# Norms, weight splits and broadcasts of a two-model fp32 forward pass, moved and regrouped

## The chip, the core and the metric

The program runs on one core of a Trainium2 chip. The metric is device time in microseconds, the median of several executions. Five engines matter here: TensorE (PE, with its weight loads shown as PEld), VectorE (DVE), ScalarE (ACT), GpSimd (POOL) and SyncE (SP), which issues most DMAs.

## What is computed

A sequence of 512 positions with 1024 channels goes through two blocks of two layers each, all in float32. Every layer mixes positions and then applies a gated feed-forward part with a short depthwise convolution:

```python
h = rmsnorm(x, pre); y = mixer(h); x = x + rmsnorm(y, post)
h = rmsnorm(x, ffn_pre); y = conv_ffn(h); x = x + rmsnorm(y, ffn_post)
```

The mixers of the first block are three attention or pooling branches with gates. Those of the second block are a convolution module and, in the last layer, dilated attention over three groups whose keys and values come from `rmsnorm(x, kv_norm_g) @ w_kv`. There the norm's gain is multiplied into the weights instead of into the activations.

## The kernel before, in words

**Products.** Every float32 product is made of three fp32r products: each operand is split in a high part (a rounded copy) and a low part (the difference), and high*high, high*low and low*high are added in PSUM (`mm3`, L329 to L331, and `mm3_rows`, L515 to L517).

**Weights.** All weights lie in one array of 500 units of 128x1024 floats in the order of use (`PLAN`). `dma_to` (L270) loads units through SP into three buffers `raw`. `split_to` (L278) splits a unit: ACT writes the high part (L299), DVE the low part (L300), into one of four buffers `w` or, for units marked keep, one of four buffers `keep`. A unit with a gain (72 units, all of the dilated stage) is first scaled in place by POOL (L296). `take_units` (L310) asks for loads up to three units ahead and for splits up to two ahead.

**Closings.** Each of the eight parts ends in `closing` (L573): the output product, then the norm, the residual addition and the next norm. It works in two halves of 256 positions, each of two tiles of 128. For half 0 it takes eight units of weights and fills four PSUM banks, then starts `norms(0)`; while that runs on DVE, ACT and POOL, PE computes half 1 with the same units; then `norms(1)` starts, and `head` begins the first six products of the next part with the normalised half 0. `head`'s first four units are keep units.

**The norm.** `norms` (L388) adds the bank to y (DVE, L398, or L401 with a bias), squares and sums it (ACT, L386), and, where there is an addition or a bias, multiplies y by the gain on POOL (L407, four 128x512 pieces per half). `rms` (L374) is a chain of twelve small DVE instructions (L379, L380, L351, then L355 to L357 three times). The residual goes into x on DVE (L413). `pre_norm` (L424) then squares x (L386), runs `rms` again, scales x into xn (ACT L441 for the first tile, DVE L437 for the second), and after a yield PE transposes xn (L448, tile `htp`) and ACT and DVE split the transposed tiles into hh and hl (L678, L679; L455, L456 without a gain), two tiles of 128 channels at a time.

**Order.** Side work is written as generators; a yield gives the time, in a clock kept while the program is built, after which the rest is issued. The framework then orders the instructions of each engine by a model of their times: among those ready in the model, the one issued first goes first. So an instruction of low priority can stand in the queue ahead of one of high priority that was not yet ready in the model. On the chip each queue runs in that order.

**Start.** `run` (L1563) issues on SP: half 0 of x, ident, vecs (562 KB of per-channel vectors), two units of weights, half 1 of x, a third unit, and small tables. Two small DVE instructions make `hb` from vecs (L1592). Then `pre_norm` of both halves and the first head.

**Dilated stage.** For each of eight heads `dilated_merge` (L1459) computes two softmax weights in small DVE and ACT steps (L1484 to L1492), yields 3.6, and PE then broadcasts them to a PSUM tile `dwb` (L362, four transposes).

Of the kernel before, what the change touches and what calls it, by code (L numbers as in the profile page):

```python
# [25 lines left out]
OP = mybir.AluOpType  # L26
# [204 lines left out]
class Kernel:  # L231
    def __init__(self, tc, t, out, stop=None):
        self.tc, self.nc, self.t, self.out, self.stop = tc, tc.nc, t, out, stop
        self.n_unit = self.n_dma = self.n_split = 0
        self.raws, self.units = {}, {}
        self.keep = None
        self.headed = []
        self.lanes, self.clock, self.ticking = [], 0.0, False
# [31 lines left out]
    def dma_to(self, n):  # L270
        while self.n_dma < min(n, len(PLAN)):
            u = self.n_dma
            raw = self.wp.tile([P, UNIT, P], F32, tag="raw", name=f"raw{u}", bufs=RAW_BUFS)
            self.nc.sync.dma_start(raw, self.t["wall"][u].rearrange("p (i m) -> p i m", m=P))
            self.raws[u] = raw
            self.n_dma += 1

    def split_to(self, n):  # L278
        nc = self.nc
        while self.n_split < min(n, len(PLAN)):  # L280
            u = self.n_split
            tiles, keep, gain = PLAN[u]
# [9 lines left out]
            if gain is not None:  # L292
                g = self.vec("kv_norm_g" if gain == "kv" else "mix_pre_g1")
                k0, n = tiles[0][2], len({k for _, _, k, _ in tiles})
                rows = raw.rearrange("p (k i) m -> p k (i m)", k=n)
                nc.gpsimd.tensor_tensor(  # L296
                    rows, rows, g[:, k0 : k0 + n, None].to_broadcast(list(rows.shape)), op=OP.mult
                )
# [3 lines left out]
            self.n_split += 1  # L302

# [70 lines left out]
    def rms(self, sums):  # L374

        nc = self.nc
        v = self.sm.tile([P, 2], F32, tag="var", name="var", bufs=2)
        y = self.sm.tile([P, 2], F32, tag="rst", name="rst", bufs=4)
# [9 lines left out]
    def norms(self, h, banks, y, add, gain, bias, pre):  # L388
# [4 lines left out]
        for i in range(2):  # L393
            for n in range(2):
# [27 lines left out]
        yield from self.pre_norm(h, pre)  # L422

    def pre_norm(self, h, gain, wait=(0.0, 0.0)):  # L424
# [9 lines left out]
        for i in range(2):  # L434
            xn.append(self.sp.tile([P, D], F32, tag="xn", name="xn", bufs=2))
            if i:
                nc.vector.tensor_scalar(  # L437
                    xn[i], self.x[:, 2 * h + i], rs[:, i : i + 1], None, op0=OP.mult
                )
            else:  # L440
                nc.scalar.activation(xn[i], self.x[:, 2 * h + i], AF.Copy, scale=rs[:, i : i + 1])  # L441
        yield NORM_SUM[h] + NORM_NEXT
        at = slice(h * HS, (h + 1) * HS)
        for f in range(0, KD, 2):
# [128 lines left out]
    def closing(self, w, l, xs, y, gain, pre, bias=None, ready=None, begun=None):  # L573
# [6 lines left out]
        with self.tc.tile_pool(name="tail", bufs=1, reuse_waits="tile") as tp:  # L580
# [8 lines left out]
            done = len(units)  # L589
            for k in range(done, KD):  # L590
# [7 lines left out]
            self.spawn(self.norms(0, banks, y, add, gain, bias, pre))  # L598
            banks = [[self.psum(tag, "mm") for tag in tags] for tags in (("a", "a"), ("a", "b"))]
            order = (4, 5, 6, 7, 0, 1, 2, 3)  # L600
            self.close_some(xs, units, banks, 1, order, every, 4, 3)
# [857 lines left out]
    def dilated_merge(self, hd):  # L1459
# [33 lines left out]
        yield 3.6  # L1493
# [69 lines left out]
    def run(self):  # L1563
        nc, tc, t = self.nc, self.tc, self.t
        with ExitStack() as st:
# [12 lines left out]
            nc.sync.dma_start(self.vecs, t["vecs"])  # L1578
# [4 lines left out]
            self.load_x(1)  # L1583
            self.dma_to(RAW_BUFS)
# [5 lines left out]
            self.hb = cst.tile([P, 48], F32, name="hb")  # L1590
            for l in range(2):
                nc.vector.tensor_scalar(  # L1592
                    self.hb[:, 24 * l : 24 * l + 24], self.vec(f"b_gate{l}"), 0.5, None, op0=OP.mult
                )
            self.new_h()
            with tc.tile_pool(name="start", bufs=1, side="right") as sp:
# [5 lines left out]
                self.keep = None  # L1602
            for n, stage in enumerate(self.stages()):
# [126 lines left out]
```

## Time and profile before

| | |
|---|---|
| median of 3 runs | 3212.48 us (3210.5 to 3213.6) |
| profiled execution | 3215.7 us, of which 3213.9 us is the span of the program's instructions |
| PE busy | 3114.8 us, 97% of the span |
| DVE, ACT, POOL busy | 1853.6, 1349.2, 423.2 us |
| mean granted TensorE clock | 0.990 |

A timeline row gives the start in us from the span's beginning, the duration, engine, line, operation, what is written <- what is read, the shape and count, and in brackets the engine's idle time before it and what ended that. Durations of matmuls overlap, since they are pipelined. The granted clock has two levels here, 1.0 (2.4 GHz) and 0.5 (1.2 GHz).

### The profile page before, as it was taken

The numbers are of one execution on the slowest core, as the hardware profiler recorded it, in microseconds if no ns is written. First come the engines' busy times: TensorE is split into PE (matmuls) and PEld (weight loads), VectorE is DVE, ScalarE is ACT, GpSimd is POOL, SyncE is SP. The second block draws the span as 40 slices with busy tenths as digits, with TensorE's granted clock in tenths as the row PEclk, the third lists the DMA queues.
The fourth block names the chain that finished last, engine by engine and source line by source line (L and its number), as shares of the span: only waits on it lengthen the run. The fifth ranks groups of instructions, "written<-read, shape, count | busy, mean of one in ns | idle before, by whom it ended". The sixth has DMA issues, their size and how long they took to land.

```text
span 3213.9 us, 40538 instructions
## 1 busy us (share of the span) xinstructions
PE 3114.8 (97%) x15764; PEld 2617.7 (81%) x15764; DVE 1853.6 (58%) x3310; ACT 1349.2 (42%) x2183; POOL 423.2 (13%) x414
## 2 busy tenths in 40 slices
PE   8999999999999999999999899999899999999998
PEld 7787878888778788888878778888788888888886
DVE  5778356446676854645467855445545545474555
ACT  4566345334456643434343244333333333353332
POOL 0223110000111322000000010000333334100001
PEclk9999999999999999999999999999999999999999
DMA  3222232232221223223334422223222222223322
GB/s 137 66 69 74 99 113 78 97 99 94 95 66 59 76 93 109 77 97 98 99 107 144 157 66 83 95 99 105 66 86 79 72 79 79 79 86 97 97 95 72
DMA packets 86687, 292.26 MB, mean 91 GB/s; under 512 B 10976, under 2 KB 15840, under 8 KB 86496
## 3 DMA queue, kind: packets, MB, share of 16 engines
q1 hardware_dynamic: 83040, 276.84, 26.2%
q10 hardware_dynamic: 3456, 12.85, 1.1%
q8 instruction: 124, 2.03, 0.3%
q14 instruction: 67, 0.55, 0.1%
HBM read 286.23 MB, written 2.10 MB: 90 GB/s over the span
## 4 chain that ended last, share of the span: by engine, by line
PE 82%; DVE 10%; ACT 4%; issue 2%; DMA 1%; SPq 1%; POOL 0%; ACTq 0%; DVEq 0%; POOLq 0%
PE mm L331 18%; PE mm L330 18%; PE mm L329 18%; PE mm L515 6%; PE mm L517 6%; PE mm L516 6%; ACT junk L386 2%; DVE w L300 2%; PE z L329 1%; PE z L331 1%; PE z L330 1%; PE htp L448 1%; DVE cacc L1279 1%; PE pt L876 1%; PE dpo L1440 1%
## 5 line engine op out<-in xcount | busy, mean ns | idle before, releaser
L329 PE MATMUL mm<-hh,w 128*128 128x512 f32 (+1 forms) x2720 | 1052.9, 387 | 0.0
L330 PE MATMUL mm<-hl,w 128*128 128x512 f32 (+1 forms) x2720 | 1036.1, 381 | 0.0
L331 PE MATMUL mm<-hh,w 128*128 128x512 f32 (+1 forms) x2720 | 1035.7, 381 | 0.0
L300 DVE TENSOR_TENSOR w<-raw,w 128x1024 fp32r<-128x1024 f32 x436 | 563.1, 1292 | 444.7 <-ACT w L299 440.3
L331 PEld LDWEIGHTS mm<-hh,w 128*128 128x128 f32 x2720 | 512.1, 188 | 96.9 <-issue 1.4
L330 PEld LDWEIGHTS mm<-hl,w 128*128 128x128 f32 x2720 | 512.8, 189 | 90.0 <-issue 2.2
L329 PEld LDWEIGHTS mm<-hh,w 128*128 128x128 f32 x2720 | 512.6, 188 | 89.8 <-issue 1.7
L299 ACT ACTIVATE w<-raw 128x1024 fp32r<-128x1024 f32 x436 | 458.9, 1053 | 237.8 <-PE mm L517 187.6
L629 DVE SCALAR_TENSOR_TENSOR cg<-mm,vecs,cg 128x511 f32<-128x511 f32 (+1 forms) x176 | 131.9, 750 | 212.8 <-ACT cg L622 209.9
L407 POOL TENSOR_TENSOR y<-y,row 128x512 f32<-128x512 f32 x40 | 53.9, 1373 | 1339.6 <-ACT junk L386 1339.6
L516 PE MATMUL mm<-w,ah 128*128 128x512 f32 x576 | 226.2, 393 | 0.0
L515 PE MATMUL mm<-w,ah 128*128 128x512 f32 x576 | 225.9, 392 | 0.0
L517 PE MATMUL mm<-w,al 128*128 128x512 f32 x576 | 225.7, 392 | 0.0
L296 POOL TENSOR_TENSOR raw<-raw,vecs 128x1024 f32<-128x1024 f32 x72 | 147.7, 2051 | 568.2 <-DMA raw<-in_wall 516.2
L629 DVE SCALAR_TENSOR_TENSOR cv<-mm,vecs,cv 128x511 f32<-128x511 f32 (+1 forms) x176 | 132.0, 750 | 100.1 <-ACT cv L622 97.3
L622 ACT ACTIVATE cg<-mm,vecs 128x512 f32<-128x512 f32 x88 | 68.7, 781 | 286.3 <-PE mm L331 286.1
L330 PE MATMUL mm<-hl,keep 128*128 128x256 f32 x512 | 144.7, 285 | 7.0 <-DVE hl L679 7.0
L331 PE MATMUL mm<-hh,keep 128*128 128x256 f32 x512 | 144.0, 283 | 0.0
L329 PE MATMUL mm<-hh,keep 128*128 128x256 f32 x512 | 143.8, 287 | 0.2
L515 PEld LDWEIGHTS mm<-w,ah 128*128 128x128 f32 x576 | 109.0, 189 | 23.3 <-issue 0.8
L516 PEld LDWEIGHTS mm<-w,ah 128*128 128x128 f32 x576 | 109.1, 189 | 22.5
L517 PEld LDWEIGHTS mm<-w,al 128*128 128x128 f32 x576 | 109.0, 189 | 22.5
(285 smaller groups left out, 4445.4 us busy)
## 6 DMA issues: line engine op xcount, KB each, us to landing
raw<-in_wall SPq DMA_DIRECT2D x500, 512.0 KB, 3.5
cw<-in_cm_mats ACTq DMA_DIRECT2D x20, 576.0 KB, 6.6
row<-in_rows SPq DMA_DIRECT2D x9, 512.0 KB, 4.2
x<-in_x SPq DMA_DIRECT2D x4, 512.0 KB, 7.2
bt<-in_rpb SPq DMA_DIRECT2D x16, 128.0 KB, 2.0
cup<-cu SPq DMA_DIRECT2D x80, 16.0 KB, 1.8
out<-x SPq DMA_DIRECT2D x4, 256.0 KB, 2.1
out<-x ACTq DMA_DIRECT2D x4, 256.0 KB, 2.1
```

What stands on the lines that cost most here:

```text
L296: nc.gpsimd.tensor_tensor(rows, rows, g[:, k0 : k0 + n, None].to_broadcast(list(rows.shape)), op=OP.mult)
L299: nc.scalar.activation(hi, raw, AF.Copy)
L300: nc.vector.tensor_tensor(lo, raw, hi.bitcast(F32), op=OP.subtract)
L329: nc.tensor.matmul(ps, wh, xh, start=first and i == 0, stop=False, **check)
L330: nc.tensor.matmul(ps, wh, xl, start=False, stop=False, **check)
L331: nc.tensor.matmul(ps, wl, xh, start=False, stop=stop, **check)
L386: self.nc.scalar.activation(junk, x, AF.Square, accum_out=total)
L515: nc.tensor.matmul(ps, xh, wh, start=first, stop=False)
L516: nc.tensor.matmul(ps, xh, wl, start=False, stop=False)
L517: nc.tensor.matmul(ps, xl, wh, start=False, stop=last)
L622: nc.scalar.activation(o, ps, AF.Identity, scale=self.vec(taps + str(k0), f), bias=self.vec(cb, f))
L629: nc.vector.scalar_tensor_tensor(o[:, to], ps[:, of], self.vec(taps + str(k), f), o[:, to], op0=OP.mult, op1=OP.add,)
```

## The change

1. Scaling by a gain moves from `split_to` to `dma_to`, right behind the load. For six units at the dilated stage's beginning (its fourth to ninth) it is done by ACT, one 128x128 tile at a time; the other 66 stay on POOL.
2. Keep units of the next head are not split before `norms(0)` has been issued (`hold`), and their ACT and DVE instructions are ordered behind the two xn instructions of half 0 (`queue_behind`, an edge in the order of one engine, without a semaphore).
3. In `norms`, the gain of the second tile is multiplied by DVE in one 128x1024 instruction behind `rms`, instead of two by POOL.
4. In the last closing, half 1 goes through the four (tile, column half) banks one after the other, and a new `last_norm` handles each tile as soon as its banks are done.
5. The yield ahead of `dwb` is 4.8 instead of 3.6.
6. At the start an 8-column copy of the first gain (`first`) is loaded in the place of vecs, vecs after half 1 of x, and `hb` is made behind the first head.

```diff
@@ dma_to
+            tiles, _, gain = PLAN[u]
+            if gain is None:
+                continue
+            g = self.vec("kv_norm_g" if gain == "kv" else "mix_pre_g1")
+            if any(at + 3 <= u < at + HEAD + 3 for at in HEADS):
+                for i, (_, _, k, _) in enumerate(tiles):
+                    self.nc.scalar.activation(raw[:, i], raw[:, i], AF.Copy, scale=g[:, k : k + 1])
+                continue
+            k0, ks = tiles[0][2], len({k for _, _, k, _ in tiles})
+            rows = raw.rearrange("p (k i) m -> p k (i m)", k=ks)
+            self.nc.gpsimd.tensor_tensor(
+                rows, rows, g[:, k0 : k0 + ks, None].to_broadcast(list(rows.shape)), op=OP.mult
+            )
@@ split_to
-            if keep and self.keep is None:
+            if keep and (self.keep is None or u >= self.hold):
                 return
...
-            nc.scalar.activation(hi, raw, AF.Copy)
-            nc.vector.tensor_tensor(lo, raw, hi.bitcast(F32), op=OP.subtract)
+            steps = [
+                nc.scalar.activation(hi, raw, AF.Copy),
+                nc.vector.tensor_tensor(lo, raw, hi.bitcast(F32), op=OP.subtract),
+            ]
+            if keep:
+                self.queue_behind(steps)
@@ norms
-                if add or bias is not None:
+                if (add or bias is not None) and i == 0:
                     nc.gpsimd.tensor_tensor(to, to, gain[:, cols], op=OP.mult)
         rs = self.rms(sums)
         for i in range(2):
             t = 2 * h + i
+            if (add or bias is not None) and i == 1:
+                nc.vector.tensor_tensor(y[:, t], y[:, t], gain, op=OP.mult)
@@ new
+    def last_norm(self, t, banks, y, gain):
...
+        for n, (to, _) in enumerate(halves):
+            nc.vector.tensor_tensor(to, to, banks[n], op=OP.add)
+            self.square(to, sums[:, 0, n : n + 1])
+        nc.vector.tensor_tensor(y[:, t], y[:, t], gain, op=OP.mult)
+        rs = self.rms(sums)
+        for n, (to, cols) in enumerate(halves):
+            nc.vector.scalar_tensor_tensor(
+                self.x[:, t, cols], to, rs[:, 0:1], self.x[:, t, cols], op0=OP.mult, op1=OP.add
+            )
+            queue = nc.scalar if n else nc.sync
+            queue.dma_start(self.out[t * P : (t + 1) * P, cols], self.x[:, t, cols])
@@ pre_norm
+            if h == 0 and self.n_unit:
+                self.behind[last.ins.engine] = last.ins
...
-                        self.hh[:, f + j, at], self.hl[:, f + j, at], pt[:, j], self.vec(gain, f + j)
+                        self.hh[:, f + j, at], self.hl[:, f + j, at], pt[:, j],
+                        self.vec(gain, f + j) if self.n_unit else self.first[:, f + j : f + j + 1],
@@ closing
+            self.hold = self.n_unit + KD - done
...
             self.spawn(self.norms(0, banks, y, add, gain, bias, pre))
+            self.hold = len(PLAN)
...
+            if pre is False:
+                for i, n in every:
+                    self.close_some(xs, units, banks, 1, order, [(i, n)], 4, 3)
+                    if n:
+                        self.last_norm(2 + i, banks[i], y, gain)
...
@@ dilated_merge
-        yield 3.6
+        yield 4.8
@@ run
-            nc.sync.dma_start(self.vecs, t["vecs"])
+            self.first = cst.tile([P, KD], F32, name="first")
+            nc.sync.dma_start(self.first, t["vecs"][:, :KD])
...
             self.load_x(1)
+            nc.sync.dma_start(self.vecs, t["vecs"])
             self.dma_to(RAW_BUFS)
```

## Rows read from the trace of the kernel before

**Rows 1.** The page's busy time of each engine, us (share of the span).

```profile
PE 3114.8 (97%) x15764; PEld 2617.7 (81%) x15764; DVE 1853.6 (58%) x3310; ACT 1349.2 (42%) x2183; POOL 423.2 (13%) x414
```

**Rows 2.** Waits of PE: who for whom, us in total, times, longest.

```profile
PE htp L448 <- ACT xn L441: 39.6, 13, 13.3
PE dwb L362 <- DVE dw L1492: 3.8, 7, 0.6
```

**Rows 3.** Timeline: a mixer's closing (474), then the first feed-forward one.

```profile
474.21 0.66 PE L448 MATMUL htp<-ident,xn 128*128 128x128 f32 x4 [0.53 <-ACT xn L441]
...
827.19 5.04 POOL L407 TENSOR_TENSOR y<-y,row 128x512 f32<-128x512 f32 x4 [385.12 <-ACT junk L386]
829.79 1.22 DVE L380 TENSOR_SCALAR var<-var 128x2 f32<-128x2 f32 x1
835.33 1.22 DVE L300 TENSOR_TENSOR keep<-raw,keep 128x1024 fp32r<-128x1024 f32 x1
...
839.54 0.17 DVE L380 TENSOR_SCALAR var<-var 128x2 f32<-128x2 f32 x1
842.73 1.15 ACT L441 ACTIVATE xn<-x,rst 128x1024 f32<-128x1024 f32 x1 [1.52 <-DVE rst L357]
843.93 0.76 PE L448 MATMUL htp<-ident,xn 128*128 128x128 f32 x4 [2.77 <-ACT xn L441]
863.17 0.39 PE L330 MATMUL mm<-hl,keep 128*128 128x256 f32 x1 [2.23 <-DVE hl L679]
872.65 0.66 PE L448 MATMUL htp<-ident,xn 128*128 128x128 f32 x4 [0.81 <-ACT xn L441]
```

**Rows 4.** Stretches: us, busy (count) of PE, PEld, DVE, ACT, POOL, clock, DMA, GB/s.

```profile
844.40:847.70 3.30, 3.30 (x10) 2.65 (x9) 1.73 (x3) 1.89 (x3) 0.00 (x0) 0.50 0.50 165
847.80:857.00 9.20, 9.15 (x49) 7.49 (x49) 6.29 (x11) 5.43 (x9) 1.30 (x1) 1.00 0.44 140
2267.80:2274.50 6.70, 5.43 (x17) 4.56 (x18) 3.84 (x5) 3.25 (x4) 3.87 (x2) 0.50 0.28 85
```

**Rows 5.** Timeline of the closing ahead of the dilated stage.

```profile
2262.07 1.92 POOL L296 TENSOR_TENSOR raw<-raw,vecs 128x1024 f32<-128x1024 f32 x1 [8.12 <-DVE nwa L356]
2262.15 2.93 DVE L300 TENSOR_TENSOR keep<-raw,keep 128x1024 fp32r<-128x1024 f32 x1
2269.07 1.11 PE L448 MATMUL htp<-ident,xn 128*128 128x128 f32 x4 [6.18 <-ACT xn L441]
2282.62 2.47 DVE L398 TENSOR_TENSOR y<-y,mm 128x512 f32<-128x512 f32 x4
2293.44 1.89 POOL L296 TENSOR_TENSOR raw<-raw,vecs 128x1024 f32<-128x1024 f32 x1
2304.80 1.11 PE L448 MATMUL htp<-ident,xn 128*128 128x128 f32 x4 [7.74 <-ACT xn L441]
```

**Rows 6.** Groups by form: count, busy us, mean ns, idle before.

```profile
L299 ACT ACTIVATE w<-raw 128x1024 fp32r<-128x1024 f32 x436 | 458.9, 1053 | 237.8 <-PE mm L517 187.6 <-DVE y L545 17.5 <-issue 15.2
L1418 ACT ACTIVATE dsm<-dsm,dst 128x128 f32<-128x128 f32 x8 | 3.1, 394 | 0.0
```

**Rows 7.** Timeline of the end.

```profile
3201.29 0.39 PE L517 MATMUL mm<-w,al 128*128 128x512 f32 x1
3208.10 2.74 DVE L413 SCALAR_TENSOR_TENSOR x<-y,rst,x 128x512 f32<-128x512 f32 x4
```

**Rows 8.** Timeline of the start, ACT, DVE and PE.

```profile
7.16 0.19 ACT L386 ACTIVATION_READ_ACCUMULATOR junk<-x 128x1 f32 x1
9.59 0.26 DVE L1592 TENSOR_SCALAR hb<-vecs 128x24 f32<-128x24 f32 x2 [8.72 <-DMA vecs<-in_vecs]
10.88 1.06 ACT L299 ACTIVATE keep<-raw 128x1024 fp32r<-128x1024 f32 x1 [3.54 <-DMA raw<-in_wall]
12.11 1.15 ACT L441 ACTIVATE xn<-x,rst 128x1024 f32<-128x1024 f32 x1 [0.17 <-DVE rst L357]
...
16.67 0.46 ACT L678 ACTIVATE hh<-htp,vecs 128x256 fp32r<-128x256 f32 x1
```

More of the change, by code (lines that the diff above doesn't have):

```diff
@@ L236, in __init__ @@
         self.keep = None
+        self.hold, self.behind = len(PLAN), {}
         self.headed = []
@@ L281, in split_to @@
             u = self.n_split
-            tiles, keep, gain = PLAN[u]
-            if keep and self.keep is None:
+            _, keep, _ = PLAN[u]
+            if keep and (self.keep is None or u >= self.hold):
                 return
@@ L291, in split_to, with queue_behind @@
             hi, lo = w[:, 0], w[:, 1]
[L292 to L298, printed above, removed]
-            nc.scalar.activation(hi, raw, AF.Copy)
-            nc.vector.tensor_tensor(lo, raw, hi.bitcast(F32), op=OP.subtract)
+            steps = [
[4 more added lines that the diff above has]
+                self.queue_behind(steps)
             self.units[u] = (hi, lo)
             self.n_split += 1
+    def queue_behind(self, steps):
+        for step in steps:
+            last = self.behind.get(step.ins.engine)
+            if last is not None:
+                self.tc.add_manual_dep(
+                    step.ins, last.name,
+                    mybir.DependencyInfo(mybir.DependencyClass.NoSync, mybir.DependencyReason.DATA),
+                    reason="weights after norms",
+                )
     def take(self, descs):
@@ L376, in rms @@
         nc = self.nc
-        v = self.sm.tile([P, 2], F32, tag="var", name="var", bufs=2)
-        y = self.sm.tile([P, 2], F32, tag="rst", name="rst", bufs=4)
+        n = sums.shape[1]
+        v = self.sm.tile([P, 2], F32, tag="var", name="var", bufs=2)[:, :n]
+        y = self.sm.tile([P, 2], F32, tag="rst", name="rst", bufs=4)[:, :n]
         nc.vector.tensor_tensor(v, sums[:, :, 0], sums[:, :, 1], op=OP.add)
@@ L422, in norms @@
         yield from self.pre_norm(h, pre)
+    def last_norm(self, t, banks, y, gain):
+        nc = self.nc
+        sums = self.sm.tile([P, 2, 2], F32, tag="sums", name="sums", bufs=4)[:, :1]
+        halves = [(y[:, t, n * S : (n + 1) * S], slice(n * S, (n + 1) * S)) for n in range(2)]
+        for n, (to, _) in enumerate(halves):
[6 more added lines that the diff above has]
+                self.x[:, t, cols], to, rs[:, 0:1], self.x[:, t, cols], op0=OP.mult, op1=OP.add
+            )
+            queue = nc.scalar if n else nc.sync
+            queue.dma_start(self.out[t * P : (t + 1) * P, cols], self.x[:, t, cols])
     def pre_norm(self, h, gain, wait=(0.0, 0.0)):
@@ L436, in pre_norm @@
             if i:
-                nc.vector.tensor_scalar(
+                last = nc.vector.tensor_scalar(
                     xn[i], self.x[:, 2 * h + i], rs[:, i : i + 1], None, op0=OP.mult
@@ L440, in pre_norm @@
             else:
-                nc.scalar.activation(xn[i], self.x[:, 2 * h + i], AF.Copy, scale=rs[:, i : i + 1])
+                last = nc.scalar.activation(
+                    xn[i], self.x[:, 2 * h + i], AF.Copy, scale=rs[:, i : i + 1]
+                )
+            if h == 0 and self.n_unit:
+                self.behind[last.ins.engine] = last.ins
         yield NORM_SUM[h] + NORM_NEXT
@@ L598, in closing @@
             self.spawn(self.norms(0, banks, y, add, gain, bias, pre))
+            self.hold = len(PLAN)
             banks = [[self.psum(tag, "mm") for tag in tags] for tags in (("a", "a"), ("a", "b"))]
             order = (4, 5, 6, 7, 0, 1, 2, 3)
+            if pre is False:
[3 more added lines that the diff above has]
+                        self.last_norm(2 + i, banks[i], y, gain)
+                self.wait()
+                self.keep = None
+                return
             self.close_some(xs, units, banks, 1, order, every, 4, 3)
@@ L1577, in run @@
             self.vecs = cst.tile([P, NVEC], F32, name="vecs")
-            nc.sync.dma_start(self.vecs, t["vecs"])
+            self.first = cst.tile([P, KD], F32, name="first")
+            nc.sync.dma_start(self.first, t["vecs"][:, :KD])
+            assert VEC["norm_mix_pre0"] == (0, KD)
             self.ones = cst.tile([P, 1], F32, name="ones")
@@ L1589, in run @@
             nc.sync.dma_start(self.pcount, t["pcount"])
[L1590 to L1594, printed above, removed]
             self.new_h()
@@ L1602, in run @@
                 self.keep = None
+            self.hb = cst.tile([P, 48], F32, name="hb")
+            for l in range(2):
+                nc.vector.tensor_scalar(
+                    self.hb[:, 24 * l : 24 * l + 24], self.vec(f"b_gate{l}"), 0.5, None, op0=OP.mult
+                )
             for n, stage in enumerate(self.stages()):
```

## The prediction

> **What bounds the kernel now.** I read the page first: PE is busy for 3114.8 of 3213.9 us [rows 1], so removing work from DVE, ACT or POOL is worth nothing by itself; at most the 99 us in which PE does not run can be won, and only where a wait of PE ends earlier. The view of waits says which: 39.6 us in 13 waits for xn ahead of the transposes, 13.3 of them at the start, and 3.8 for the weights of dwb [rows 2]. The remainder is made of waits that the change does not touch, and of the tail behind the last matmul.
>
> The timeline of a feed-forward closing shows why xn is late. The same instruction of the norm, L380 on 128x2, takes 0.17 us in the second norm and 1.22 in the first, where POOL's four multiplications run from 827.19 for 5.04 us [rows 3]: DVE's small instruction ends when one of POOL's ends. L351 behind it goes the same way, so the first norm loses 2 x 1.05 = 2.1 us. In the same chain stand keep splits of the next head (835.33, and two more), 1.22 us each [rows 3]. PE reaches the transposes at 841.16 and waits 2.77 us; later it waits 2.23 for hl, because DVE is again held behind POOL, and 0.81 for the second xn [rows 3]. Three closings look like this (both feed-forward parts of the first block, and the convolution module).
>
> The framework orders each queue by a model of times, so a keep split in the chain, which the model knows, and a lock by POOL, which it may not know, are different things. In the two closings of the first block's mixers, where POOL multiplies nothing but keep splits do stand in the chain, PE waits only 0.53 us for the first xn [rows 3]. I conclude that PE's order is already arranged around the keep splits, and that the wait is mainly the lock.
>
> A wait costs more than itself: behind the 2.77 us the granted clock is 0.50 for 3.4 us. There PE starts 10 matmuls in 3.30 us, against 49 in 9.2 at full clock [rows 4]; 3.4 x (1 - 3.03/5.33) makes 1.4 us lost.
>
> **The change part by part.**
>
> *Feed-forward closings (3).* POOL keeps two of four multiplications, which end about 2.5 us after the first begins, at 829.7, just ahead of L380: the lock of 2.1 us goes, and the 2.77 becomes about 0.6. DVE gains one 128x1024 multiplication per half. No row has it; the nearest is L413 at the end, four 128x512 updates in 2.74 [rows 7], so 1.3 for two, which I take. Its bounds are 1.22 (a split of the same size [rows 3]) and 2.9 (a split that meets POOL [rows 5]). The keep splits, four ACT instructions of 1.05 and four DVE instructions of 1.22, leave the first norm and land in the following 14 us, where hh, hl and four more splits already stand. What they free in the chain is about the 1.3 put in, plus a little.
> What is late next is the second norm. Its inputs come 2.2 us earlier (3.6 where the 1.4 of slow clock go too). Its own length changes by -2.4 (lock, two instructions), +1.3 (multiplication) and 0 to +1.2 (a split pushed into it), so about -0.5. PE then reaches the second transposes some 3 us ahead of xn, where it waited 0.81 or nothing before. I expect the slow clock behind that wait, 1.4 us, in all three. The gains are 3.6 + 0.5 - 1.4 less the margin PE had: 2.2, 0.9 and 2.1 in the three, together **5.2**. Ends: 0 (the splits fill DVE) and 12 (no slow clock, no split in the chain).
>
> *The closing ahead of the dilated stage.* Here POOL also scales weights. Its 1.92 us at 2262.07 stretch a split from 1.22 to 2.93, and PE waits 6.18, then 7.74 [rows 5]; the slow clock follows the first for 6.7 us with 17 matmuls [rows 4] and the second too. With the fourth to ninth unit on ACT, no scaling runs during the first norm. The first wait falls from 6.18 to about 0.6, and the slow clock behind it (6.7 x 0.43 = 2.9 us of work) goes, so the second norm gets its inputs 8.5 to 10 us earlier, near 2276. It is 19.6 us long from its last addition to PE's transposes (2285.09 to 2304.80 [rows 5]), of which locks take about 7. Two scalings, of the tenth and eleventh unit, stay on POOL (2293.44 is the later one [rows 5]) and may lock it again. ACT's price for one unit: eight instructions of 128x128, each at most 0.394 [rows 6], so 3.2 at most, and no less than the 1.05 of one instruction over all columns [rows 6]; I take 0.3 x 8 = 2.4, since neighbouring ACT instructions overlap by about 0.1. Six units make 14 us of ACT in some 28, beside 17 us of other work there: tight, but the last two or three units are not needed until the head is over. They delay the squares by 1 to 3 us. So 19.6 - 7 + 1.3 + 2 makes 16, with up to 3.8 of lock by the two that stay: xn at 2292 to 2296, against 2304.8; PE's own work, which ended at 2297.06, ends at 2289 to 2291.5. I take 2293.8: **11.0**, ends 4 and 15.
> The rows show that a split of two SBUF inputs and a small scalar instruction wait for POOL [rows 3, 5]. The Trainium skill, GPSIMD Engine Reference, section Key points, says that GpSimd shares its SBUF interfaces with VectorE and contends with instructions in a two-port mode or with two SBUF inputs. By that rule the moved multiplication (y and gain, both in SBUF) can be held as well, and the two remaining scalings hold the second norm in full, 3.8 us: the sum would then be about 2 us smaller.
>
> *The other three closings with a head* (two mixers, the dilated one) change by the keep splits alone: 0, ends -3 and +2. Cover: the model's order leaves PE other matmuls while keep splits wait; if hh and hl slip behind two splits each, that cover is gone (the rival below).
>
> *dwb.* PE waits 3.8 us in 7 places, the longest 0.6 [rows 2], the last 0.5 of it at the end of the stage, where there is no other work. With 1.2 us more of matmuls ahead, six waits go: **3.1**, ends 0 and 3.8. Nothing waits for dwb but y of its head, used after the stage.
>
> *Scalings issued one unit earlier (66 on POOL).* POOL already starts them when the load lands; they need no split before them: 0, ends -3 and +2, since POOL's small scalings of probabilities stand in the same queue, and PE waits for those.
>
> *The end.* Now: the last bank, four additions, four squares, `rms` with the lock of 2.1 [rows 3], four updates in 2.74. After: one addition 0.7, one square 0.8, multiplication 1.3, `rms` without a lock 2.4 (as 9.76 to 12.07 at the start), two updates 1.4. From the last matmul's end at 3201.68 this comes to 3208.3, against 3210.84 [rows 7]: **2.5**, ends 1.5 and 4. The output DMAs behind it are the same.
>
> *The start.* The squares are summed at 7.35; DVE stands at hb until vecs land at 9.56 [rows 8]. Without that, rms ends at 9.7 instead of 12.07. But ACT's queue has a keep split, waiting for its load until 10.88, ahead of xn [rows 8]. vecs' 562 KB, 1.4 us at the spacing of its neighbours, leave the front of SP's queue, so that load lands at about 9.5 and the next at 10.8. If one split stays ahead of xn, xn starts at 10.6 (1.5 earlier); if both do, at about 12.0 (0.1); if none, at 9.7 (2.4). I take **1.0**, ends -0.5 and 3. Only the first two channel tiles use `first`; the others wait for vecs, which now land behind half 1 of x, at about 14.8. Their first user ran at 16.67 [rows 8], so 1.9 us of cover. hb's two instructions of 0.26 move to where DVE is free. heads, rot and pcount are behind vecs as before.
>
> **Sum.** 5.2 + 11.0 + 3.1 + 2.5 + 1.0 = 22.8 us off the profiled execution's 3215.7 us (1.8 around the span): 3192.9. The median of the runs, 3212.5, is 3.2 lower, so the forecast is **3189.7 us**.
>
> **Rivals.**
> *A: the second norm takes it back.* All closings are bound by the second xn, whose length grows by the multiplication and a split as much as it loses, and the slow clock follows each wait. For: the 0.81 us wait there shows that it is already even with PE [rows 3]. Against: locks of 2.4 and 7 us that go. Then the closings give 5 instead of 16.2: 3201.
> *B: more comes out.* No slow clock behind the second transposes (the wait of 2.23 us at 863.17 [rows 3] brought none), and xn ahead of both splits at the start: 5 + 4 + 1.5 more, about 3179.
> *C: slower.* In each of the seven closings with a head, the four keep splits now stand between the pieces of hl. Each of the four rounds of transposes takes one more split, 1.22 on DVE [rows 3], so the last hl comes 4.9 us later: 7 x 4.9 = 34 us, and 3189.7 + 34 = 3224. It decides when more than about 2 us of that falls at a point where the model has no other matmul for PE. For: DVE has only some 5 us free there. Against: four keep splits start 3 us earlier with xn, and PE has six independent products.
> *D: the change in order does not happen* (the edges bind nothing that the model would not do anyway). The locks still go; the keep splits stay in the chain: 1 to 2 us less, 3191, inside the forecast.
>
> **Numbers.** Forecast (with D) 0.68, spread 3182 to 3199 by the ends above; A 0.17; B 0.10; C 0.05. The range of 8 in 10 takes in the forecast, most of A and half of B: 3178 to 3203. 0.2% is 6.4 us, about what a measurement of this kernel can tell from no change. Over 3206 are C and a tail of A: faster 0.92, same 0.04, slower 0.04.
>
> **What would show it.** Right: L380 of the first norms at 0.2; waits for the first xn near 0.6 in four closings, no keep split between x and xn; PE's wait for the second xn at 1 to 4 us; POOL's scalings gone from 2262 to 2284; no dwb wait but the last; some 6.6 us from the last matmul to the last update; hb gone from the start. Wrong: waits for hl of more than 1 us ahead of the heads (C), ACT waiting for raw between units (the scalings block it), a first hh waiting for vecs, or new waits of PE for dsm in the dilated stage.

## The result, and the profile after

The kernel after takes 3189.4 us (median of four runs, 3188.1 to 3191.9) against 3213.0 (3210.5 to 3213.8; three of these four runs gave the 3212.5 that stands ahead of the prediction): a ratio of 0.9929, 95% interval 0.9914 to 0.9945. The forecast was 3189.7. The experiments show that this is the right sum with its large terms wrong.

The page's busy time of each engine, kernel after [rows 1]:

```profile
PE 3113.7 (98%) x15764; PEld 2617.2 (82%) x15764; DVE 1836.5 (58%) x3333; ACT 1361.1 (43%) x2231; POOL 378.1 (12%) x386
```

The waits of PE of the kernel after, by waiting instruction (us in total, times, longest) [rows 2]:

```profile
PE htp L494 <- ACT xn L483: 23.9, 14, 13.9
PE mm L351 <- ACT hh L735: 4.4, 9, 0.8
PE htp L494 <- DVE hl L736: 3.7, 5, 1.4
PE dwb L384 <- DVE dw L1549: 0.6, 1, 0.6
```

PE does the same work; its waits shrank. Those for xn fell from 39.6 to 23.9 us, of which 13.9 are the start, and those for dwb from 3.8 to 0.6. The waits for hl were 10.4 us in five places before, three of them of 2.2 to 2.5 ahead of products (863.17 [rows 3] is one); now they are 3.9 in six. New are nine short waits for hh. In the kernel after, L448 is L494, xn's L441 is L483, the splits L299 and L300 are L307 and L308, L379, L380 and L351 are L402, L403 and L373, and POOL's L407 and L296 are L430 and L288. L435 is the moved multiplication.

The first feed-forward closing, timeline (start, duration, engine, instruction, idle before it) [rows 3]:

```profile
828.50 2.56 POOL L430 TENSOR_TENSOR y<-y,row 128x512 f32<-128x512 f32 x2 [388.61 <-ACT junk L409]
830.99 1.21 DVE L435 TENSOR_TENSOR y<-y,row 128x1024 f32<-128x1024 f32 x1
832.13 0.16 DVE L403 TENSOR_SCALAR var<-var 128x2 f32<-128x2 f32 x1
842.33 0.66 PE L494 MATMUL htp<-ident,xn 128*128 128x128 f32 x4 [0.95 <-ACT xn L483]
873.01 1.09 PE L494 MATMUL htp<-ident,xn 128*128 128x128 f32 x8 [0.72 <-ACT xn L483]
```

L403 takes 0.16 where L380 took 1.22, the wait for the first xn is 0.95 instead of 2.77, and the second stays at 0.72. The closing ahead of the dilated stage [rows 5]:

```profile
2259.58 0.66 PE L494 MATMUL htp<-ident,xn 128*128 128x128 f32 x4 [0.94 <-ACT xn L483]
2286.92 0.33 PE L494 MATMUL htp<-ident,xn 128*128 128x128 f32 x1 [0.82 <-ACT xn L483]
2290.55 1.90 POOL L288 TENSOR_TENSOR raw<-raw,vecs 128x1024 f32<-128x1024 f32 x1 [16.44 <-DVE hl L502]
```

Waits of 6.18 and 7.74 us are now 0.94 and 0.82; of the scalings left on POOL three end by 2239.8, and the next starts only at 2290.55, behind both norms. But the mixer's closing, where PE waited for little but 0.53 us for xn [rows 3], got worse. Its timeline in the kernel after, and under it a row of the view of stretches (the last three numbers: granted clock, DMA share, GB/s):

```profile
475.92 1.06 ACT L307 ACTIVATE keep<-raw 128x1024 fp32r<-128x1024 f32 x1 [0.38 <-DMA raw<-in_wall]
483.01 1.06 ACT L307 ACTIVATE w<-raw 128x1024 fp32r<-128x1024 f32 x1 [1.09 <-DMA raw<-in_wall]
485.86 0.63 PE L494 MATMUL htp<-ident,xn 128*128 128x128 f32 x4 [1.37 <-DVE hl L736]
487.78 0.80 PE L351 MATMUL mm<-hh,keep 128*128 128x256 f32 x2 [0.58 <-ACT hh L735]
```
```profile
487.66:491.07 3.41, 3.29 (x15) 3.29 (x16) 3.24 (x11) 1.12 (x4) 0.00 (x0) 0.50 0.60 214
```

ACT stands at splits whose raw has not landed, hh and hl queue behind them, PE waits 1.37 and 0.58 us, and the granted clock is 0.50 for 3.41 us. No such stretch was there before.

Where the span's 23.8 us come from, by the start of the same ACT instruction in each trace (us; gain against before). The last two columns are two of the experiments below, the kernel after without part 2 of the change (hold and edges) and the kernel before with that part alone:

| up to | before | after | gain | without hold | hold alone |
|---|---|---|---|---|---|
| first mixer's matmuls | 458.53 | 456.36 | 2.2 | 2.4 | 1.1 |
| behind its closing | 508.25 | 509.52 | -1.3 | 2.4 | -2.7 |
| behind the first feed-forward closing | 906.64 | 905.34 | 1.3 | 8.1 | -4.6 |
| behind the second mixer's closing | 1346.42 | 1346.98 | -0.6 | 9.0 | -6.7 |
| behind the second feed-forward closing | 1748.94 | 1747.90 | 1.0 | 13.5 | -9.6 |
| end of the convolution's own work | 1847.09 | 1848.54 | -1.4 | 13.2 | -9.6 |
| behind the convolution's closing | 2031.42 | 2028.23 | 3.2 | 19.6 | -10.6 |
| behind the closing ahead of the dilated stage | 2336.09 | 2315.91 | 20.2 | 36.6 | -11.1 |
| end of the dilated stage | 2740.73 | 2716.24 | 24.5 | 40.3 | -10.8 |
| behind its closing | 2860.61 | 2839.06 | 21.6 | 40.3 | -12.9 |
| end of the span | 3213.9 | 3190.1 | 23.8 | 42.4 | -13.0 |

A single entry for the kernel after is good to about 2 us early and 4 late: three experiments below (all scalings on POOL, the old yield, the old end) have its order of instructions up to 2260 us, and they came to the second row's place 1.1 to 2.2 us sooner and behind the convolution's closing 1.6 to 4.2. In them too the mixers' closings lose against before, 1.4 to 2.6 us each, but the clock of 0.50 at 487 is in none of the three. And the profiled run of the kernel after was the slowest of its four, that of the kernel without the hold the fastest: the two spans are 18.6 us apart, the medians 13.0.

### The profile page after: what moved, and what is told of

Its sections match the earlier page's. It is cut to its first block, busy times and chain, and to the rows that moved or that the text cites. A ratio compares the mean times of both kernels' runs of the same rounds, so it can differ in the third digit from the quotient of the medians.

```text
span 3190.1 us, 40545 instructions
## 1 busy us (share of the span) xinstructions
PE 3113.7 (98%) x15764; PEld 2617.2 (82%) x15764; DVE 1836.5 (58%) x3333; ACT 1361.1 (43%) x2231; POOL 378.1 (12%) x386
## 5 line engine op out<-in xcount | busy, mean ns | idle before, releaser
L351 PE MATMUL mm<-hh,w 128*128 128x512 f32 (+1 forms) x2720 | 1052.3, 387 | 0.0
L308 DVE TENSOR_TENSOR w<-raw,w 128x1024 fp32r<-128x1024 f32 x436 | 570.0, 1308 | 433.1 <-ACT w L307 428.6
L351 PEld LDWEIGHTS mm<-hh,w 128*128 128x128 f32 x2720 | 512.2, 188 | 89.3 <-issue 1.7
L307 ACT ACTIVATE w<-raw 128x1024 fp32r<-128x1024 f32 x436 | 458.9, 1053 | 236.7 <-PE mm L564 172.5
L288 POOL TENSOR_TENSOR raw<-raw,vecs 128x1024 f32<-128x1024 f32 x66 | 132.5, 2008 | 545.8 <-DMA raw<-in_wall 511.2
L430 POOL TENSOR_TENSOR y<-y,row 128x512 f32<-128x512 f32 x18 | 23.3, 1311 | 1358.0 <-ACT junk L409 1358.0
L351 PE MATMUL mm<-hh,keep 128*128 128x256 f32 x512 | 144.4, 290 | 4.4 <-ACT hh L735 4.4
```

Of the source, the lines that this page charges most:

```text
L288: self.nc.gpsimd.tensor_tensor(rows, rows, g[:, k0 : k0 + ks, None].to_broadcast(list(rows.shape)), op=OP.mult)
L307: nc.scalar.activation(hi, raw, AF.Copy),
L351: nc.tensor.matmul(ps, wh, xh, start=first and i == 0, stop=False, **check)
```

## The experiments

"Theory" in each expectation is what I held before that run. All ratios are against the kernel before.

### Part 2 taken out, and part 2 alone

```diff
@@ closing
-            self.hold = self.n_unit + KD - done
@@ split_to
-            if keep:
-                self.queue_behind(steps)
```

> The kernel after without the hold and without the edges behind the norms; all else stays. Theory (holding the keep splits back is a net loss: the mixers' closings and the w_o closing lost 3.4, 2.1 and 3.4 us, the conformer's stage 1.1, and the gains of the other closings come from POOL and ACT): the four places come back, about 3189.4 - 10 = 3180 us, and the waits for the first xn in the mixers' closings are 0.5 us again with no slow clock at 487. Rival 1 (what the prediction said: keep splits out of the chain pay for the moved multiplication in the three feed-forward and convolution closings and in the dilated one): those lose 1.2 us or more for each split in the chain, 4 x 2.4 = 10 us, and the mixers give 0: about 3199. Rival 2 (the edges bind nothing that the order would not do anyway): 3189, within 2.

3176.3 us, ratio 0.9883 (0.9866 to 0.9899): 13.0 us faster than the kernel after, and the last experiment's kernel, which is its equal but for the start, cannot be told from it. It is called the fastest kernel below. Waits of PE:

```profile
PE htp L492 <- ACT xn L481: 21.6, 12, 14.3
```

Waits for hh are gone altogether, and 7.3 us of waits for xn are left beside the start's 14.3. Rival 1, the prediction's own view, falls. The loss was not in the mixers alone: by the table the three feed-forward and convolution closings give 5.7, 4.5 and 6.4 us without the hold, where the kernel after got 2.6, 1.6 and 4.6.

The kernel before with the same lines added:

> The kernel before with the hold and the edges alone; none of the other parts. Theory (a net loss): the mixers and w_o lose 3.4 + 2.1 + 3.4 us as in the kernel after, and the closings in which POOL locks DVE gain at most 1.2 us each: 3213.0 + 9 - 4, about 3218 us, between 3215 and 3223. Rival 1 (the keep splits were the wait): the three closings with 2 to 3 us of wait and the dilated one gain 2.4 us each and the mixers nothing: about 3203. Rival 2: 3213, within 2.

3228.3 us, ratio 1.0040 (1.0025 to 1.0055): 13 us slower by the ratio, 15 by the medians, more than the 5 expected. The direction is the theory's; that closings with locks (DVE instructions that are held until one of POOL's ends) would gain 1.2 us each is wrong: the three feed-forward and convolution closings lost 1.0 to 2.9 by the table, and the one ahead of the dilated stage gained nothing. Its waits of PE for xn:

```profile
PE htp L466 <- ACT xn L457: 50.6, 14, 14.8
```

The longest, 14.8 us, is that for the second xn ahead of the dilated stage, 7.74 before [rows 5]: there, from 2290 to 2310, nine instructions of POOL stand among the second norm's on DVE, and five of the small instructions (L395 to L372), 0.16 us alone, take 1.2 to 1.9.

### Hold or edges

The kernel after with one of the two edits of above alone. Hold only:

```diff
@@ split_to
-            if keep:
-                self.queue_behind(steps)
```

Edges only:

```diff
@@ closing
-            self.hold = self.n_unit + KD - done
```

> The kernel after with the hold (keep splits written down only behind the first norm) but without the edges behind xn. It cost 13 us to have both. Theory (the edges cost it: four keep splits in a row behind xn, ahead of hh, hl and the stream splits): all of it comes back, 3176 us, between 3173 and 3180, and keep splits run ahead of xn again. Rival (the late place in the program costs it, since the planner takes instructions in the order in which they are written where it has a choice): 3189, within 3. Half and half would be 3183.

> The kernel after with the edges alone: the keep splits are written down as early as in the kernel before. An edge then goes to the xn of the norm that was written last, so the splits written ahead of the first norm have an edge to the xn of the closing before, which binds nothing. Theory (the edges cost it): only the splits written behind the norm are bound; if those are the four of the head, 3189 within 3; if they are fewer, in between. Rival (the late place costs it): 3176, within 3.

Hold only: 3178.2 us, ratio 0.9893 (0.9876 to 0.9911). Edges only: 3185.8, ratio 0.9916 (0.9900 to 0.9932). So 11.2 of the 13 us go with the edges, and they cost 9.5 even where the splits are written early. The traces say why: with the hold only, the four splits of the first mixer's closing run between 461 and 471, as in the fastest kernel; with the edges only, one runs there and three behind xn at 470; with both, all four run from 470 on. ACT's waits for the loads of stream units (us in total, times, longest), in the kernel after:

```profile
ACT w L307 <- DMA raw<-in_wall: 16.4, 18, 2.1
```

In the fastest kernel, without part 2:

```profile
ACT w L307 <- DMA raw<-in_wall: 1.8, 2, 1.6
```

With the hold only:

```profile
ACT w L307 <- DMA raw<-in_wall: 1.2, 2, 0.7
```

With the edges only:

```profile
ACT w L307 <- DMA raw<-in_wall: 14.9, 20, 1.8
```

They wait some 15 us in the two kernels with edges, and below 2 in the two without. Three raw buffers serve keep and stream units in turn; a keep split that is held keeps its buffer, so the loads behind it start late, and in ACT's queue hh waits behind the split that waits. In the first mixer's closing SP issues no load of weights from 444.6 to 472.4 in the kernel after; in the fastest kernel the next one goes out at 464.5. That this chain makes up all of the cost is not shown; a fourth raw buffer, which would separate it from the queueing itself, was not tried.

### The multiplication back on POOL

```diff
-                if (add or bias is not None) and i == 0:
+                if add or bias is not None:
...
-            if (add or bias is not None) and i == 1:
-                nc.vector.tensor_tensor(y[:, t], y[:, t], gain, op=OP.mult)
```

> The kernel after with POOL's four multiplications by the gain back in the first and second norm, and none on DVE. Theory (the wait was POOL's lock): the three closings lose what they gained, 2.7 + 1.7 + 3.2 = 7.6 us, the dilated closing some 3 us of its 17, about 3189.4 + 10.6 = 3200 us; L378 and L379 on 128x2 take 1.2 us again in the first norm, and PE waits 2 to 3 us for the first xn there. Rival (the keep splits in the chain were the wait, and the edges removed it): DVE is freed of 1.3 us per half, so within 2 us of 3189 or a little faster.

3209.0 us, ratio 0.9986 (0.9977 to 0.9996): 19.7 us lost, nearly twice the expected 10.6. The first feed-forward closing again:

```profile
827.00 5.07 POOL L430 TENSOR_TENSOR y<-y,row 128x512 f32<-128x512 f32 x4 [387.18 <-ACT junk L409]
829.61 1.23 DVE L403 TENSOR_SCALAR var<-var 128x2 f32<-128x2 f32 x1
841.94 0.65 PE L492 MATMUL htp<-ident,xn 128*128 128x128 f32 x4 [2.96 <-ACT xn L481]
861.44 1.27 DVE L402 TENSOR_TENSOR var<-sums 128x2 f32<-128x2 f32 x1
862.75 1.23 DVE L403 TENSOR_SCALAR var<-var 128x2 f32<-128x2 f32 x1
```

The keep splits are out of the chain here, and PE still waits 2.96 us: the lock was the wait, as the prediction concluded. And the second norm is locked as well (861.44, 862.75), so each closing pays twice.

This edit and that of the first experiment, so without hold and edges:

> No hold, no edges, and POOL's four multiplications by the gain back in each norm; so the start, the end, the scalings on ACT and the later broadcasts stay. It gives the price of the moved multiplication without the edges beside it. Theory (locks by POOL, as before, no matter where the keep splits stand): the three feed-forward and convolution closings lose the 6.2 + 4.4 + 6.4 us by which they are faster than in the kernel before, the dilated closing some 5: 3176.3 + 22, about 3198 us. Rival (the prediction's sizes, 2.2 + 0.9 + 2.1 and a part of the dilated closing): about 3184.

3195.6 us, ratio 0.9950 (0.9933 to 0.9966): 19.3 lost by the medians, 21.5 by the ratios. So this part is worth 18 to 22 us with or without part 2, the largest of the change. PE in the first feed-forward closing of this kernel:

```profile
842.18 0.69 PE L490 MATMUL htp<-ident,xn 128*128 128x128 f32 x2 [2.76 <-ACT xn L479]
861.18 0.39 PE L350 MATMUL mm<-hl,keep 128*128 128x256 f32 x1 [2.14 <-DVE hl L731]
```

In the fastest kernel, where no row has a wait for that xn or that hl:

```profile
841.49 0.66 PE L492 MATMUL htp<-ident,xn 128*128 128x128 f32 x4
```

So the wait for the first xn comes with POOL's multiplications, whether the keep splits stand in the chain (2.76, and 2.77 before) or not (2.96), and without them it is 0.95 with the splits held and nothing with the splits in the chain. The wait for hl of before (2.23) comes back with them too, and is not there without them.

### All scalings on POOL

```diff
-            if any(at + 3 <= u < at + HEAD + 3 for at in HEADS):
-                for i, (_, _, k, _) in enumerate(tiles):
-                    self.nc.scalar.activation(...)
-                continue
```

> The kernel after with the weights' scaling of the fourth to ninth unit on POOL too, so all on POOL, issued with the load as in the kernel after. Theory (in the closing ahead of the dilated stage the scalings on POOL were the locks, and the gain of 17.0 us there is mostly theirs): the closing loses 8 to 13 us, about 3200 us, with PE waits for xn of 3 us or more at 2269 to 2305 and slow clock behind them. Rival (the moved multiplication and the held splits gave it): the closing keeps all but 2 or 3 us, about 3192.

3202.6 us, ratio 0.9962 (0.9947 to 0.9977): 13.2 lost, all ahead of the dilated stage. DVE there, with POOL's three scalings of the same time, and PE's next transposes:

```profile
2276.28 1.23 DVE L304 TENSOR_TENSOR w<-raw,w 128x1024 fp32r<-128x1024 f32 x1 [2.88 <-ACT w L303]
2277.42 1.86 DVE L398 TENSOR_TENSOR var<-sums 128x2 f32<-128x2 f32 x1
2279.20 1.21 DVE L431 TENSOR_TENSOR y<-y,row 128x1024 f32<-128x1024 f32 x1
2280.34 1.86 DVE L399 TENSOR_SCALAR var<-var 128x2 f32<-128x2 f32 x1
...
2276.36 8.72 POOL L284 TENSOR_TENSOR raw<-raw,vecs 128x1024 f32<-128x1024 f32 x3
...
2296.20 1.12 PE L490 MATMUL htp<-ident,xn 128*128 128x128 f32 x4 [9.02 <-ACT xn L479]
```

The two engines take turns: a DVE instruction of 1.2 us runs undisturbed while POOL stands, and the small one behind it is held for the 1.9 us of POOL's scaling. With the edit of the first experiment added, so without hold and edges:

> No hold, no edges, and all scalings of weights on POOL, issued with the load. With the edges this cost 13.5 us in the closing ahead of the dilated stage, in one wait of 9.0 for the second xn and one of 2.4 for hl. Theory (POOL's scalings lock DVE's norms there, edges or not): 3176.3 + 12, about 3188 us, with a wait of 5 us or more for the second xn. Rival (the edges pushed the keep splits into the second norm, where they met the scalings; without them the norms get by): 3178 to 3181.

3183.9 us, ratio 0.9915 (0.9901 to 0.9930): 7.6 lost by the medians, between the two expectations, with waits of 4.45 and 5.65 us for the two xn. The locks are there without the edges. Whether the edges add to them is open: by the medians the loss is 13.2 with edges and 7.6 without, by the ratios 10.6 and 10.3.

### The three small parts

The old yield, the old end and the old start, each put back by itself in the kernel after. The yield:

```diff
-        yield 4.8
+        yield 3.6
```

> The kernel after with the old 3.6 in place of 4.8 ahead of the broadcasts of the stream weights. The prediction priced this part at 3.1 us, the two traces laid beside each other at 4.3: about 3193, the waits for dwb back at 0.5 to 0.6 in seven places in the dilated stage. Rival (the time of those waits is made up elsewhere in the stage): 3189.5, within 1.

3192.1 us, ratio 0.9936 (0.9919 to 0.9954): 2.7 lost, against the prediction's 3.1, and dwb's waits are back:

```profile
PE dwb L384 <- DVE dw L1549: 3.9, 7, 0.6
```

The end (all of the last half goes to `norms`):

```diff
-            if pre is False:
-                for i, n in every:
...
-                return
```

> The kernel after with the old end: the last half's norm over both tiles at once. The prediction priced this part at 2.5 us, the two traces laid beside each other at 2.8: about 3192, with the last update ending 9.2 us behind the last matmul or somewhat less, since POOL now multiplies one tile only. Rival (the one multiplication on DVE, not the tile by tile order, gave most of it): 3190, within 1.

3192.2 us, ratio 0.9938 (0.9922 to 0.9953): 2.8 lost, against 2.5.

The start (hb's two instructions also go back ahead of the norm, and `first` is left out):

```diff
+            nc.sync.dma_start(self.vecs, t["vecs"])
...
             self.load_x(1)
-            nc.sync.dma_start(self.vecs, t["vecs"])
```

> The kernel after with the old start: vecs loaded whole ahead of raw, hb's two instructions ahead of the first norm, no small load. The prediction priced this part at 1.0 us (-0.5 to 3), the two traces laid beside each other at 2.1: about 3191.5, the first transposes at 13.3 instead of 13.9 us and a wait of PE of 1.8 us near 33 us again. Rival (the late first transposes cancel the earlier loads): 3189.4, within 1.

3188.6 us, ratio 0.9929 (0.9914 to 0.9944): nothing lost, the rival's figure. ACT and PE at the start of the kernel after, timeline:

```profile
8.31 1.06 ACT L307 ACTIVATE keep<-raw 128x1024 fp32r<-128x1024 f32 x1 [0.98 <-DMA raw<-in_wall]
9.57 1.06 ACT L307 ACTIVATE keep<-raw 128x1024 fp32r<-128x1024 f32 x1 [0.20 <-DMA raw<-in_wall]
10.93 0.63 ACT L409 ACTIVATE junk<-x 128x512 f32<-128x512 f32 x1 [0.30 <-DMA x<-in_x]
12.73 1.15 ACT L483 ACTIVATE xn<-x,rst 128x1024 f32<-128x1024 f32 x1 [0.33 <-DVE rst L379]
...
13.93 0.90 PE L494 MATMUL htp<-ident,xn 128*128 128x128 f32 x3 [13.93 <-ACT xn L483]
```

PE with the old start:

```profile
11.84 0.90 PE L494 MATMUL htp<-ident,xn 128*128 128x128 f32 x3 [11.84 <-ACT xn L483]
...
32.80 0.63 PE L494 MATMUL htp<-ident,xn 128*128 128x128 f32 x4 [1.72 <-DVE hl L736]
```

In the kernel after, the norm no longer waits for vecs, but two keep splits and squares of half 1 came in ahead of xn, whose loads land earlier too. The old start reaches the transposes 2.1 us sooner and gives 1.7 back in one wait. That the table shows a gain of 2.2 up to the first mixer's matmuls is due to the run of before: its hb started at 9.59 [rows 8], with vecs; in this kernel, which issues the same loads in the same order, at 8.11, and it came to the table's first row at 456.08, as soon as the kernel after (456.36).

### A start with edges

The fastest kernel, with the edges at the start alone (the edit is shown against the kernel after; the hold is out as well).

```diff
@@ split_to
-            if keep:
+            if u < HEAD:
                 self.queue_behind(steps)
@@ pre_norm
-            if h == 0 and self.n_unit:
+            if h == 0 and not self.n_unit:
```

> No hold and no edges in the closings, as in the fastest kernel so far (3176.3), but edges at the one norm that the change left out: at the start the keep splits come behind the first xn. There they stood in the chain (two of 1.05 and 1.22 us between the pieces of the first norm), and PE had no other work. Theory (an edge pays where PE has nothing else to do, and costs where it has): xn at 9.6 instead of 13.1, the first transposes at 10.8 instead of 14.3, and 2 us of that left at 46 us: 3174. Rival (the splits of the first keep tiles, now 2 us later, hold up the first products, and the loads of raw with them): 3176 to 3178, with a wait of PE near 17 or 33 us.

Ratio 0.9876 (0.9856 to 0.9896), against 0.9883 without: no difference that can be told. The first transposes came at 10.93 instead of 14.33, and of these 3.4 us 0.3 were left at 46. The rival's figure is right; a wait near 17 or 33 us, its sign, did not come: the view has one wait of 0.2 us for hh. PE's matmuls in this kernel, timeline:

```profile
12.84 0.58 PE L351 MATMUL mm<-hh,keep 128*128 128x256 f32 x1
20.09 0.41 PE L353 MATMUL mm<-hh,keep 128*128 128x256 f32 x1
20.65 0.28 PE L351 MATMUL mm<-hh,keep 128*128 128x256 f32 x1
```

In the kernel without the edges:

```profile
17.73 0.41 PE L349 MATMUL mm<-hh,keep 128*128 128x256 f32 x1
18.29 0.28 PE L349 MATMUL mm<-hh,keep 128*128 128x256 f32 x1
```

A 128x256 matmul takes some 0.4 us where the granted clock is 0.50 (0.41 at 488.37 of the kernel after, within the stretch above), and 0.28 at 1.00. PE left the long one after 20.1 us with the early start and after 17.7 with the late one, over 9 and over 3 us behind its first transposes. By 22 us the two kernels had started 49 and 48 matmuls, transposes included. So the early work was done at the length of half the clock (the trace's own record of the clock begins, with 1.00, only at 20.5 and 18.2 us). And it had gaps: the eight products that start from 12.84 to 16.04 are 0.46 us apart on average, the next ones 0.21, which makes some 1.7 us, up to half of the 3.4. A part of the rival's reason, products held up at the start, is thus not excluded.

This kernel also shows why equal closings differ from run to run. The second norm ahead of the dilated stage, in this kernel:

```profile
2267.22 1.90 POOL L288 TENSOR_TENSOR raw<-raw,vecs 128x1024 f32<-128x1024 f32 x1 [11.02 <-DVE w L308]
2267.77 1.36 DVE L402 TENSOR_TENSOR var<-sums 128x2 f32<-128x2 f32 x1 [1.48 <-ACT junk L409]
2270.47 1.89 POOL L288 TENSOR_TENSOR raw<-raw,vecs 128x1024 f32<-128x1024 f32 x1 [1.35 <-DVE nwa L377]
2270.55 1.83 DVE L379 SCALAR_TENSOR_TENSOR rst<-nwa,rst 128x2 f32<-128x2 f32 x1
...
2274.20 0.69 PE L494 MATMUL htp<-ident,xn 128*128 128x128 f32 x2 [3.96 <-ACT xn L483]
```

In the fastest kernel, whose engines have the same instructions in the same order from 61 us on:

```profile
2266.68 1.90 POOL L288 TENSOR_TENSOR raw<-raw,vecs 128x1024 f32<-128x1024 f32 x1 [10.12 <-DVE w L308]
2271.54 1.93 POOL L288 TENSOR_TENSOR raw<-raw,vecs 128x1024 f32<-128x1024 f32 x1 [2.96 <-DMA dmove<-in_dmove]
...
2272.16 0.55 PE L492 MATMUL htp<-ident,xn 128*128 128x128 f32 x3 [1.57 <-ACT xn L481]
```

In the first, POOL's two scalings meet the chain and hold two small instructions for 1.36 and 1.83 us; in the second, one ended as the chain began (2268.58) and the other came behind it.

## Why the prediction was right, and where it was not

Each part's worth, by the runs in which it was undone, beside the prediction's term:

| part | predicted | undone, us | worth |
|---|---|---|---|
| half of POOL's multiplications to DVE | 5.2 with the splits, and a share of the 11.0 | 3209.0 | 19.7 |
| scalings to ACT | the rest of the 11.0 | 3202.6 | 13.2 |
| later broadcasts | 3.1 | 3192.1 | 2.7 |
| the end | 2.5 | 3192.2 | 2.8 |
| the start | 1.0 | 3188.6 | -0.8 |
| hold and edges | 0 in three closings, a small plus in the others | 3176.3 | -13.0 |
| sum | 22.8 | | 24.6 |

The result is 23.7 (3213.0 - 3189.4). A worth is a difference of two medians, and those of the kernel before, measured beside each experiment, lie between 3211.3 and 3214.5. By the ratios, which take that out, the column reads 18.3, 10.6, 2.2, 2.9, 0.0 and -14.8, and the result 22.8. Each edit also makes the planner order the engines anew, so a part's worth is that of the part with its order.

**Right.** That the wait for the first xn was "mainly the lock" and that it falls to about 0.6 (0.95 measured); that POOL's scalings would leave both norms; dwb and the end, each within 0.4 us.

**Wrong: the keep splits.** The step is "The other three closings with a head ... change by the keep splits alone: 0". Holding the splits costs 1.4 to 3.5 us, by the table and the three traces with the same order, in six of the seven closings with a head, and 13 us by the medians. Ahead of the dilated stage it costs nothing or even gives: that closing gained 16.8 to 17.0 us in the kernel after and with the old yield, end or start, and 17.0, 12.5 and 12.1 in the three without edges in the closings (fastest kernel, hold only, edges at the start). Rival C had the place, splits between the pieces of hl, and sized it at 34 us; part of the cost comes by a way that C did not name, the raw buffers. Two of the prediction's signs of being wrong were there: waits for hl above 1 us (1.37 at 485.86) and ACT waiting for raw between units, though the held splits and not the scalings cause it. "What they free in the chain is about the 1.3 put in" fails too: without edges the splits stand in the chain, and the feed-forward closings are faster.

**Wrong: the feed-forward closings' size.** Undoing the multiplication costs more than 5.2 in three closings plus a share of the fourth. The step "2.2, 0.9 and 2.1 in the three" let PE come to the second transposes "some 3 us ahead of xn" and took 1.4 us of slow clock behind that wait from each. The wait came out at 0.7, and the granted clock stayed at 1.00. The step went by PE's order of before, but the planner made another: from the first transposes of half 0 to those of half 1 PE starts 163 matmuls before, 191 in the kernel after and 167 in the fastest kernel, in 28.7, 30.7 and 24.2 us (first feed-forward closing). Without the hold the three give 5.7, 4.5 and 6.4 us by the table, 3.5 to 4.3 more than predicted; the 2.3 of wait and the 1.4 of slow clock that did not come make 3.7.

**Wrong by a size: the closing ahead of the dilated stage.** 11.0 predicted (4 to 15), 17.0 by the table (20.2 - 3.2). The failing step is that two scalings "may lock it again". They ran at 2290.55 and later, behind the norm. The second norm took 14.5 us from its last addition (ended at 2272.44) to the transposes, not 16, and the expected wait of some 3 us, with slow clock behind it, was 0.82 with none. The last experiment shows that this can come out otherwise: 12.1 in a closing of the same edits but the hold and the edges.

**Wrong: the start.** "If one split stays ahead of xn": both did, and two squares of half 1. "If both do ... 0.1" was the case named for it, and about right.

The first two rows of the table are worth 32.9 us, where the steps for them made 16.2; the hold took 13.0 of the rest back, the start 1.8. That errors of 17 and 15 us cancelled to within 2 us is luck: of the large terms only the total was predicted.

## What to carry to other kernels

In this kernel a chain of small instructions held by another engine's was the thing to free; instructions that the planner had put into its gaps did harm when they were moved out by hand, since they held buffers and went on to stand in front of something else. Ask of each held instruction which buffer it keeps, and which load that stops. And price the parts of a change by undoing each: a total that agrees shows nothing of its terms, here 13 us were to be had by leaving one part out.

## What the runs showed of the hardware

**The lock goes by turns.** With all scalings on POOL ahead of the dilated stage, DVE's 128x1024 multiplication of two SBUF operands took 1.21 us among POOL's scalings (2279.20 above), and the 128x2 instructions behind it took 1.86, whether of two inputs (L398) or of one (L399). The prediction feared for the multiplication; here it is what follows it that pays. The Trainium skill, SBUF — State Buffer, section Who interferes with whom, says that the order of issue decides who blocks, and not the shape of the operation; the trace agrees: the long operation with two SBUF operands ran its usual 1.21 us, the short one behind it 1.86 instead of 0.16, and a split of the same size that began 0.33 us behind one of POOL's scalings (2264.36) took 2.65.

**Equal programs differ by several us at one lock.** The two second norms shown last differ by 2.4 us in PE's wait (3.96 and 1.57), in programs whose order differs at the start alone; by the start of the same ACT instruction behind the closing it is 4.9 us. Behind the longer wait the granted clock was 0.50 from 2273.3 to 2280.2; in the other trace it stayed at 1.00 there.

**A start that is earlier is not always time won.** PE's first 3.4 us were lost again, at half the matmul rate and in gaps between the first products, as the start with edges shows.

**Loads of the same order land differently.** With equal issues ident landed at 8.12 us in the run of before and at 5.77 in that with the old start, and the loads behind it 1.5 us apart. So a gain of some 2 us at the start that one profile shows needs a second run.
